# Retention heads in pairs: the turned results joined behind the next pair's steps, one inverse root for two heads

## The chip, the cores and the metric

The kernel runs on one core of one Trainium2 chip. The metric is the device time of one execution in microseconds (us). Before the change it is 2228.16 us, the median of three runs (2228.16, 2228.16 and 2229.72 us). About 0.2% of it, 4.5 us, is what a measurement of this kernel can tell from no change.

## The reference

One decoder layer over 256 tokens of width 2048: a half feed-forward, two token mixers side by side (retention and windowed attention), a second half feed-forward, and a gated embedding, each closed by a layer norm. The change lies in the retention mixer. What it computes:

```python
def reference(x, p, positions, ln_g, ...):
...
        rq = rotary(rq.reshape(B, S, RET_HEADS, RET_DK), positions, RET_DK, RET_THETA)
        rk = rotary(rk.reshape(B, S, RET_HEADS, RET_DK), positions, RET_DK, RET_THETA) * (RET_DK ** -0.5)
        rv = rv.reshape(B, S, RET_HEADS, RET_DV)
        ro = head_group_norm(retention_chunkwise(rq, rk, rv), ret_gn_g[i]).astype(h.dtype)
        ret_branch = (jax.nn.silu(rg) * ro) @ w_ret_out[i]
...
# retention_chunkwise: o_t = sum_{s<=t} gamma_h^(t-s) (q_t . k_s) v_s
...
def head_group_norm(o, g):
    B, S = o.shape[0], o.shape[1]
    mu = jnp.mean(o, axis=-1, keepdims=True)
    var = jnp.mean(jnp.square(o - mu), axis=-1, keepdims=True)
    y = (o - mu) * lax.rsqrt(var + GN_EPS)
    return y.reshape(B, S, -1) * g.astype(jnp.float32)
```

There are 8 retention heads; a head has 128 columns of query and key and 256 of value. Everything is float32.

## The kernel before, in words

Each matrix product is made exact by splitting: a weight chunk of 128 by 1024 numbers comes in by a DMA (`r...`, issued by SyncE), ScalarE rounds it to a high part (`h...`, L162), VectorE subtracts for the low part (`l...`, L164), and TensorE runs three matmuls for each product (L510 to L512): low times high, high times high, high times low. `fill` (L394) loads and splits chunks some way ahead of the chunk that TensorE is at; in the stage of this change the split is four chunks ahead.

Small work is laid between the chunks. `side` is a list of jobs, and `run_side` (L445) takes one job off it behind each chunk, after `fill` has issued the splits. The same call moves `lazy` on, which here prepares sums of later weights (`uf_gu`, `vf_gu`, L372 to L384), and `slow`, which makes a table of angles (`rota`, `triga`). Every engine runs its instructions in the order in which this code issues them, so a job's place in `side` is its place in each engine's queue.

The retention stage walks over four blocks of the gate (L1566, h = 0, 2, 4, 6). A block is one call of `paired_out` (L652): eight chunks of `w_in_f2`, summed into the two banks `rg`. Behind these 32 chunks the heads' jobs run. For a head h:

- `ret1` (L1475): TensorE multiplies queries and keys into the bank `rs`; VectorE multiplies by the decay into `rsc` (L1483, L1484).
- `ret1b` (L1488): ScalarE and VectorE split `rsc` into `rsp` (L113, L114).
- `ret2` (L1495): TensorE multiplies `rsp` by the values into the bank `ro`, nine matmuls (L1504); VectorE takes mean and variance into `gmv` (L1511, L1512).
- `ret2b` (L1516): `rsqrt` (L688), ten small instructions of VectorE, makes the inverse root; two more (L1525) write the normed head to `ron`.

For a pair c of heads:

- `ret2c`: VectorE multiplies `ron` by the gate (L1533).
- `ret3`: ScalarE copies the words of `ron` apart (`wro`, L227). `ret3a`: SyncE issues the DMA transpose `mro` (L231).
- `ret3b` (L1543): ScalarE joins what the transpose delivered into `ron0t`, `ron1t` and so on (L238) and scales it by the norm's weight (L1552); VectorE makes the low part (L1553). The results `rett` are first read at 1237.6 us of the span, by the output product of the retention branch, over 220 us after the last of them is written.

In `side` a pair of heads takes ten places: five for `ret1` to `ret2b`, and five for `ret2c`, `ret3`, `ret3a`, an empty one and `ret3b`, ahead of the next pair's five. A block takes off eight. So the list falls two further behind with every block: `ret1` of head 2 comes behind the sixth chunk of the second block, that of head 4 behind the last chunk of the third, and the jobs of the last pair run beside the value chunks `av` and the first attention features `aqk`.

PSUM has eight banks, taken in turn (L82); a block and its pair ask for six: two `rg`, two `rs`, two `ro`.

Of the kernel before, what the change touches and what calls it, by code (L numbers as in the profile page):

```python
# [8 lines left out]
F32 = mybir.dt.float32  # L9
# [4 lines left out]
ALU = mybir.AluOpType  # L14
PSUM = bass.MemoryType.PSUM

P = 128
# [3 lines left out]
HR, DK, DV = 8, 128, 256  # L21
# [4 lines left out]
GN_EPS = 1e-5  # L26
# [44 lines left out]
def layer(ctx: ExitStack, tc: tile.TileContext, io):  # L71
    nc = tc.nc
    sync, act, dve, pool, pe = nc.sync, nc.scalar, nc.vector, nc.gpsimd, nc.tensor
# [4 lines left out]
    small = ctx.enter_context(tc.tile_pool(name="small", bufs=3))  # L78
# [6 lines left out]
    def banks(name):  # L85
        return [bank(name + str(j)) for j in range(2)]

    def slot(shape, dt, name):
        return slots.tile(shape, dt, tag="slot", name=name)
# [351 lines left out]
    side = []  # L441
    lazy, slow = [], []
    idle = lambda: None
# [244 lines left out]
    def rsqrt(dst, var, n, eps):  # L688

        v = small.tile([P, 2, n], F32, tag=f"nv{n}", name="nv")
        dve.scalar_tensor_tensor(
            v, var[:, None, :].broadcast_to([P, 2, n]), eps, newton[:, :, None].broadcast_to([P, 2, n]),
            ALU.add, ALU.mult,
        )
        s = small.tile([P, n], I32, tag=f"ns{n}", name="ns", bufs=2)
        dve.tensor_scalar(s, v[:, 0].bitcast(I32), 1, None, ALU.logical_shift_right)
        y = small.tile([P, n], I32, tag=f"ny{n}", name="ny", bufs=2)
        dve.tensor_scalar(y, s, -1.0, float(0x5F3759DF - 2**31), ALU.mult, ALU.add)  # L700

        def square(cur, w, name):
            b = small.tile([P, n], F32, tag=f"nb{n}", name=name)
            if n == 1:
                dve.tensor_scalar(b, cur, cur, w, ALU.mult, ALU.mult)
            else:
                dve.tensor_tensor(b, cur, cur, ALU.mult)
                dve.tensor_tensor(b, b, w, ALU.mult)
# [634 lines left out]
    def mixers(ht, norm, residual, keepers, away):  # L1343
# [123 lines left out]
        for blk in range(2, 4):  # L1467
            ps = banks(f"rv{blk}")
# [4 lines left out]
        keep = {}  # L1473
# [21 lines left out]
        def ret2(h):  # L1495
            def f():
                s = keep.pop(("s", h))
                v = [x[:, :, h % 2 * DV : h % 2 * DV + DV] for x in rv[h // 2]]
                ps = bank(f"ro{h}").rearrange("p (a b) -> p a b", a=2)
                for t, blks in ((0, ((0, 0),)), (1, ((P, 0), (S, 1)))):  # L1500
                    for col, tk in blks:
                        at = slice(col, col + P)
                        for a, b in ((1, 0), (0, 0), (0, 1)):
                            pe.matmul(  # L1504
                                ps[:, t, :DV], s[:, a, at], v[b][:, tk],
                                start=(a, tk) == (1, 0) and col != S, stop=b == 1 and (t, col) in ((0, 0), (1, S)),
                            )
                st = small.tile([P, 2, 6], F32, tag="gst", name=f"gst{h}")
                mv = small.tile([P, 2, 2], F32, tag="gmv", name=f"gmv{h}")
                for t in range(2):  # L1510
                    dve.bn_stats(st[:, t], ps[:, t, :DV])  # L1511
                    dve.bn_aggr(mv[:, t], st[:, t])  # L1512
                keep["m", h] = ps, mv
            return f

        def ret2b(h):  # L1516
            def f():
                ps, mv = keep.pop(("m", h))
                rs = small.tile([P, 2], F32, tag="grs", name=f"grs{h}")
                rsqrt(rs, mv[:, :, 1], 2, GN_EPS)  # L1520
                if h % 2 == 0:
                    keep["o", h // 2] = slot([P, 2, 512], F32, f"ron{h}")
                o = keep["o", h // 2][:, :, h % 2 * DV : h % 2 * DV + DV]
                for t in range(2):
                    dve.tensor_scalar(  # L1525
                        o[:, t], ps[:, t, :DV], mv[:, t, 0:1], rs[:, t : t + 1], ALU.subtract, ALU.mult
                    )
            return f

        def ret2c(c):  # L1530
            def f():
                o = keep.pop(("o", c))
                dve.tensor_tensor(o, o, gate_v[c], ALU.mult)  # L1533
                keep["t", c] = Turn(o, f"ro{c}")
            return f

        def ret3(c):
            return lambda: keep["t", c].part()

        def ret3a(c):  # L1540
            return lambda: keep["t", c].move()

        def ret3b(c):  # L1543
            def f():
                raw = slot([P, 4, S], F32, f"ron{c}t")
                keep.pop(("t", c)).join(raw)
                for j in range(4):
                    if j % 2 == 0:
                        ret_t.append(slot([P, 2, 512], F32R, f"rett{len(ret_t)}"))
                    gk = gn[:, 4 * c + j : 4 * c + j + 1]  # L1550
                    hi, lo = ret_t[-1][:, j % 2, :S], ret_t[-1][:, j % 2, S:]
                    act.mul(hi, raw[:, j], gk)  # L1552
                    dve.scalar_tensor_tensor(lo, raw[:, j], gk, hi, ALU.mult, ALU.subtract)  # L1553
            return f

        both = lambda a, b: lambda: (a(), b())

        def two_heads(h):
            side.append(ret1(h))
            side.append(both(ret1b(h), ret1(h + 1)))  # L1560
            side.append(both(ret1b(h + 1), ret2(h)))
            side.append(both(ret2b(h), ret2(h + 1)))
            side.append(ret2b(h + 1))

        two_heads(0)
        for h in range(0, HR, 2):  # L1566
            ps = banks(f"rg{h}")
            paired_out(("w_in_f2", grp), KD, rhs, ps)
            grp += 2
            g = slot([P, 2, 512], F32, f"rgs{h}")  # L1570
            for t in range(2):
                act.activation(g[:, t], ps[t], AF.Silu)
            gate_v.append(g)
            c = h // 2
            side.extend((ret2c(c), ret3(c), ret3a(c), idle, ret3b(c)))
            if h + 2 < HR:
                two_heads(h + 2)
        aq = [slot([P, 4, S], F32, f"aq{j}") for j in range(2)]
        akv = slot([P, 4, S], F32, "akv")
        ps = banks("av")  # L1580
# [119 lines left out]
        for j in range(4):  # L1700
# [6 lines left out]
            ps = banks(f"gt{j}")  # L1707
# [26 lines left out]
        for j in range(4):  # L1734
            v = sig[4 + j]
# [8 lines left out]
        for b in range(2):  # L1744
# [3 lines left out]
            for n in range(2):  # L1748
                j = 2 * b + n
# [31 lines left out]
        ps = banks("mo2")  # L1781
# [4 lines left out]
        ps = banks("mo3")  # L1786
# [326 lines left out]
```

## Time and profile before

| What | Value |
|---|---|
| Median of three runs | 2228.16 us |
| The profiled execution's own time | 2227.58 us |
| Its span, from the first to the last instruction | 2225.5 us |
| TensorE (PE) busy | 2210.3 us, 99% of the span |
| VectorE (DVE) busy | 2027.8 us, 91% |
| ScalarE (ACT) busy | 1473.8 us, 66% |
| DMA, mean over the span | 259 GB/s |
| The retention stage (first `rg` to last `rg` matmul) | 865.8 to 970.0 us |

The profiled execution's time is 2.1 us over its span. With TensorE busy for 99% of the span, a change of the time is one of two things: TensorE waits less or more, or its clock is granted differently. Both are read by stage, since sums over the span hide them.

### The profile page before, as it was taken

To read this page: it belongs to the slowest core of one execution; us is meant where nothing else is said; L and a number is where in the kernel's file an instruction comes from. 1 tells how busy PE (TensorE), PEld (TensorE's weight loads), DVE (VectorE), ACT (ScalarE), POOL (GpSimd) and SP (SyncE) were. 2 spreads that over 40 slices of the span, in tenths; PEclk is the share of its full clock that TensorE was granted. 3 is DMA by queue.
4 is the path that set the end of the run, shared out by engine and by line. 5 is a ranking of instruction groups with operands and counts; after the bars stand their busy time and mean duration, and the time that the engine had idled before them with its cause. 6 is when DMAs were issued, how large, how long until landed. Compare 5 with 4: busy or idle time off the path is not lost.

```text
span 2225.5 us, 28896 instructions
## 1 busy us (share of the span) xinstructions
PE 2210.3 (99%) x9980; PEld 1826.6 (82%) x9980; DVE 2027.8 (91%) x2660; ACT 1473.8 (66%) x1706; POOL 48.3 (2%) x62
## 2 busy tenths in 40 slices
PE   9999999999999999999999999999999999999998
PEld 7888888888888888888788888888888878888887
DVE  6999999999988997999999888779999999999877
ACT  5877777777565555657866567466767678765553
POOL 0000000000000000000000000000000000000000
PEclk9999999999999999999999999999999999999999
DMA  9979889977686789876976578888899899767771
GB/s 315 275 224 267 248 245 262 251 234 245 217 304 234 254 272 317 260 279 227 295 235 221 183 210 327 311 302 261 292 311 309 293 261 274 216 238 240 282 289 71
DMA packets 315754, 576.00 MB, mean 259 GB/s; under 512 B 107084, under 2 KB 112076, under 8 KB 315608
## 3 DMA queue, kind: packets, MB, share of 16 engines
q1 hardware_dynamic: 305992, 543.79, 73.1%
q0 software_dynamic: 7632, 27.79, 6.7%
q10 hardware_dynamic: 1984, 2.58, 0.3%
q8 instruction: 78, 1.28, 0.2%
q14 instruction: 68, 0.56, 0.1%
HBM read 490.20 MB, written 33.55 MB: 235 GB/s over the span
## 4 chain that ended last, share of the span: by engine, by line
PE 87%; DVE 5%; DMA 4%; ACT 2%; issue 2%; SPq 0%; ACTq 0%; DVEq 0%; POOLq 0%
PE f2g L510 2%; PE f2g L511 2%; PE f2g L512 2%; PE f1g L512 2%; PE f1g L511 2%; PE f1g L510 2%; PE f1u L511 2%; PE f1u L512 2%; PE f1u L510 2%; PE f2u L512 2%; PE f2u L510 2%; PE f2u L511 2%; PE aqk L461 2%; PE f1d L511 1%; PE f1e L510 1%
## 5 line engine op out<-in xcount | busy, mean ns | idle before, releaser
L164 DVE TENSOR_TENSOR lf_gu<-rf_gu,hf_gu 128x1024 fp32r<-128x1024 f32 x123 | 145.2, 1218 | 18.9 <-ACT hf_gu L162 18.1
L164 DVE TENSOR_TENSOR lw_in_f<-rw_in_f,hw_in_f 128x1024 fp32r<-128x1024 f32 x124 | 148.6, 1218 | 10.3 <-ACT hw_in_f L162 9.5
L162 ACT CAST hf_gu<-rf_gu 128x1024 fp32r<-128x1024 f32 x123 | 123.6, 1049 | 26.5 <-DMA rf_gu<-in_f_gu 24.9
L164 DVE TENSOR_TENSOR lf_down<-rf_down,hf_down 128x1024 fp32r<-128x1024 f32 x96 | 115.8, 1219 | 24.5 <-ACT hf_down L162 19.1
L284 ACT CAST huf_gu<-uf_gu 128x1024 fp32r<-128x1024 f32 x83 | 87.3, 1052 | 76.4 <-DVE uf_gu L280 68.9
L293 ACT CAST hvf_gu<-vf_gu 128x1024 fp32r<-128x1024 f32 x83 | 87.5, 1054 | 76.1 <-DVE vf_gu L289 65.2
L162 ACT CAST hw_in_f<-rw_in_f 128x1024 fp32r<-128x1024 f32 x124 | 125.3, 1048 | 7.1 <-DMA rw_in_f<-in_w_in_f 3.3
L162 ACT CAST hf_down<-rf_down 128x1024 fp32r<-128x1024 f32 x96 | 98.5, 1050 | 30.4 <-DMA rf_down<-in_f_down 12.3
L298 DVE TENSOR_TENSOR lvf_gu<-vf_gu,hvf_gu 128x1024 fp32r<-128x1024 f32 x83 | 100.9, 1216 | 0.0
L296 DVE TENSOR_TENSOR luf_gu<-uf_gu,huf_gu 128x1024 fp32r<-128x1024 f32 x83 | 100.9, 1215 | 0.0
L287 DVE TENSOR_TENSOR lf_gu<-rf_gu,hf_gu 128x1024 fp32r<-128x1024 f32 x83 | 100.9, 1215 | 0.0
L277 ACT CAST hf_gu<-rf_gu 128x1024 fp32r<-128x1024 f32 x83 | 86.8, 1045 | 9.8 <-DMA rf_gu<-in_f_gu 6.7
L510 PE MATMUL f1g<-hf_gu,xt 128*128 128x512 f32 x223 | 87.0, 390 | 0.5 <-ACT hf_gu L113 0.5
L512 PE MATMUL f1g<-lf_gu,xt 128*128 128x512 f32 x223 | 87.1, 391 | 0.1
L511 PE MATMUL f1g<-hf_gu,xt 128*128 128x512 f32 x223 | 86.8, 389 | 0.0
L510 PE MATMUL f2g<-hf_gu,ht 128*128 128x512 f32 x196 | 76.4, 390 | 0.0
L512 PE MATMUL f2g<-lf_gu,ht 128*128 128x512 f32 x196 | 76.3, 389 | 0.0
L511 PE MATMUL f2g<-hf_gu,ht 128*128 128x512 f32 x196 | 76.3, 389 | 0.0
L510 PE MATMUL f1u<-hf_gu,xt 128*128 128x512 f32 x180 | 70.0, 389 | 0.0
L512 PE MATMUL f1u<-lf_gu,xt 128*128 128x512 f32 x180 | 70.0, 389 | 0.0
L511 PE MATMUL f1u<-hf_gu,xt 128*128 128x512 f32 x180 | 70.0, 389 | 0.0
L182 POOL DMA_DIRECT2D lf_gu<-rf_gu x37 | 32.1, 869 | 1637.2 <-DMA rf_gu<-in_f_gu 1049.0
(1640 smaller groups left out, 7318.5 us busy)
## 6 DMA issues: line engine op xcount, KB each, us to landing
rf_gu<-in_f_gu SPq DMA_DIRECT2D x362, 512.0 KB
rf_down<-in_f_down SPq DMA_DIRECT2D x176, 512.0 KB
rw_in_f<-in_w_in_f SPq DMA_DIRECT2D x148, 512.0 KB
lf_gu<-rf_gu POOLq DMA_DIRECT2D x37, 512.0 KB, 8.6
rw_rv<-in_w_rv SPq DMA_DIRECT2D x32, 512.0 KB
rw_ret<-in_w_ret SPq DMA_DIRECT2D x32, 512.0 KB
rw_mix<-in_w_mix SPq DMA_DIRECT2D x32, 512.0 KB
rw_pg<-in_w_pg SPq DMA_DIRECT2D x32, 512.0 KB
```

The lines of the kernel that those rows point to most:

```text
L162: act.copy(c.hi, c.raw)
L164: dve.tensor_tensor(c.lo, c.raw, c.hi, ALU.subtract)
L277: act.copy(a.hi, a.raw)
L284: act.copy(uh, u)
L287: dve.tensor_tensor(a.lo, a.raw, a.hi, ALU.subtract)
L293: act.copy(vh, v)
L296: dve.tensor_tensor(ul, u, uh, ALU.subtract)
L298: dve.tensor_tensor(vl, v, vh, ALU.subtract)
L461: pe.matmul(ps[f], hi[:, kk, f * P : (f + 1) * P], rhs(k), start=k == 0, stop=k == n_k - 1,)
L510: pe.matmul(o, al, bh, start=first, stop=False)
L511: pe.matmul(o, ah, bh, start=False, stop=False)
L512: pe.matmul(o, ah, bl, start=False, stop=self.left == 0)
```

## The change

`ret3b` of a pair no longer stands ahead of the next pair's steps. It goes into the last of the next pair's five places, together with the new `ret2b`. The empty place behind `ret3a` goes too, so that a pair takes eight places, as many as a block takes off. Only the last pair, which has no next one, keeps the empty place and `ret3b` behind it.

`ret2b` is called once for a pair: it waits until both heads' `ret2` are done, takes one inverse root of four columns where two of two columns were taken, and then norms both heads. The tile `gmv` holds both heads' means and variances.

```diff
                 st = small.tile([P, 2, 6], F32, tag="gst", name=f"gst{h}")
-                mv = small.tile([P, 2, 2], F32, tag="gmv", name=f"gmv{h}")
+                if h % 2 == 0:
+                    keep["v", h // 2] = small.tile([P, 4, 2], F32, tag="gmv", name=f"gmv{h}")
+                mv = keep["v", h // 2]
                 for t in range(2):
                     dve.bn_stats(st[:, t], ps[:, t, :DV])
-                    dve.bn_aggr(mv[:, t], st[:, t])
-                keep["m", h] = ps, mv
+                    dve.bn_aggr(mv[:, h % 2 * 2 + t], st[:, t])
+                keep["m", h] = ps
             return f
 
-        def ret2b(h):
+        def ret2b(c):
             def f():
-                ps, mv = keep.pop(("m", h))
-                rs = small.tile([P, 2], F32, tag="grs", name=f"grs{h}")
-                rsqrt(rs, mv[:, :, 1], 2, GN_EPS)
...
+                mv = keep.pop(("v", c))
+                rs = small.tile([P, 4], F32, tag="grs", name=f"grs{c}")
+                rsqrt(rs, mv[:, :, 1], 4, GN_EPS)
+                o = keep["o", c] = slot([P, 2, 512], F32, f"ron{c}")
+                for e in range(2):
+                    ps = keep.pop(("m", 2 * c + e))
+                    for t in range(2):
+                        j = 2 * e + t
+                        dve.tensor_scalar(
+                            o[:, t, e * DV : e * DV + DV], ps[:, t, :DV], mv[:, j, 0:1], rs[:, j : j + 1],
+                            ALU.subtract, ALU.mult,
+                        )
             return f
...
-        def two_heads(h):
+        def two_heads(h, last=idle):
             side.append(ret1(h))
             side.append(both(ret1b(h), ret1(h + 1)))
             side.append(both(ret1b(h + 1), ret2(h)))
-            side.append(both(ret2b(h), ret2(h + 1)))
-            side.append(ret2b(h + 1))
+            side.append(ret2(h + 1))
+            side.append(both(ret2b(h // 2), last))
...
-            side.extend((ret2c(c), ret3(c), ret3a(c), idle, ret3b(c)))
+            side.extend((ret2c(c), ret3(c), ret3a(c)))
             if h + 2 < HR:
-                two_heads(h + 2)
+                two_heads(h + 2, ret3b(c))
+            else:
+                side.extend((idle, ret3b(c)))
```

VectorE's queue around the first job of head 4 (`rsc4`), before. `lw_in_f2_12_7` is the low part of the third block's last chunk, `14_0` to `14_3` are chunks of the fourth block, `rett2` and `rett3` belong to `ret3b` of heads 2 and 3, `uf2_gu` and `vf2_gu` are the sums of later weights:

```order
L164 TENSOR_TENSOR lw_in_f2_12_7_8296<-rw_in_f2_12_7_8129,hw_in_f2_12_7_8295 128x1024
L164 TENSOR_TENSOR lw_in_f2_14_0_8317<-rw_in_f2_14_0_8172,hw_in_f2_14_0_8316 128x1024
L372 TENSOR_TENSOR uf2_gu_4_0_4_8326<-rf2_gu_4_0_4_8217,rf2_gu_4_1_4_8219 128x512
L373 TENSOR_TENSOR uf2_gu_4_0_4_8326<-rf2_gu_4_1_4_8219 128x512
L164 TENSOR_TENSOR lw_in_f2_14_1_8351<-rw_in_f2_14_1_8238,hw_in_f2_14_1_8350 128x1024
L164 TENSOR_TENSOR lw_in_f2_14_2_8369<-rw_in_f2_14_2_8277,hw_in_f2_14_2_8368 128x1024
L1553 SCALAR_TENSOR_TENSOR rett2_8377<-ron1t_8374,gn_79,rett2_8377 128x256 x2
L1553 SCALAR_TENSOR_TENSOR rett3_8382<-ron1t_8374,gn_79,rett3_8382 128x256 x2
L376 TENSOR_TENSOR vf2_gu_4_0_4_8327<-rf2_gu_4_0_4_8217,uf2_gu_4_0_4_8326 128x512
L377 TENSOR_TENSOR vf2_gu_4_0_4_8327<-vf2_gu_4_0_4_8327,rf2_gu_4_0_4_8217 128x512
L164 TENSOR_TENSOR lw_in_f2_14_3_8403<-rw_in_f2_14_3_8299,hw_in_f2_14_3_8402 128x1024
L1483 TENSOR_TENSOR rsc4_8411<-rs4_8408,dec2_7284 128x256
```

The same place of VectorE's queue after the change:

```order
L384 TENSOR_TENSOR lvf2_gu_3_0_5_8033<-vf2_gu_3_0_5_8029,hvf2_gu_3_0_5_8032 128x1024
L164 TENSOR_TENSOR lw_in_f2_12_7_8263<-rw_in_f2_12_7_8131,hw_in_f2_12_7_8262 128x1024
L1483 TENSOR_TENSOR rsc4_8271<-rs4_8268,dec2_7284 128x256
L1484 TENSOR_TENSOR rsc4_8271<-rs4_8268,dec2_7284 128x128
L164 TENSOR_TENSOR lw_in_f2_14_0_8287<-rw_in_f2_14_0_8191,hw_in_f2_14_0_8286 128x1024
L114 TENSOR_TENSOR rsp4_8292<-rsc4_8271,rsp4_8292 128x384
L1483 TENSOR_TENSOR rsc5_8298<-rs5_8295,dec2_7284 128x256
L1484 TENSOR_TENSOR rsc5_8298<-rs5_8295,dec2_7284 128x128
```

`rsc4` has moved up by four chunks, to right behind the split of `12_7`, and `rett2` and `rett3` no longer stand ahead of it.

ScalarE's queue at the same place, before (`ron1t` is the joining of heads 2 and 3, `rgs4` the gate of heads 4 and 5, `rsp4` the high part that head 4's second product needs):

```order
L162 CAST hw_in_f2_14_0_8316<-rw_in_f2_14_0_8172 128x1024
L162 CAST hw_in_f2_14_1_8350<-rw_in_f2_14_1_8238 128x1024
L162 CAST hw_in_f2_14_2_8368<-rw_in_f2_14_2_8277 128x1024
L238 COPY ron1t_8374<-mro1_8322 128x2x4x128 x2
L1552 ACTIVATE rett2_8377<-ron1t_8374,gn_79 128x256 x2
L1552 ACTIVATE rett3_8382<-ron1t_8374,gn_79 128x256 x2
L375 CAST huf2_gu_4_0_4_8328<-uf2_gu_4_0_4_8326 128x1024
L162 CAST hw_in_f2_14_3_8402<-rw_in_f2_14_3_8299 128x1024
L1572 ACTIVATE rgs4_8414<-rg40_8154 128x512
L1572 ACTIVATE rgs4_8414<-rg41_8155 128x512
L162 CAST hw_in_f2_14_4_8431<-rw_in_f2_14_4_8320 128x1024
L113 CAST rsp4_8437<-rsc4_8411 128x384
```

And after the change:

```order
L162 CAST hw_in_f2_14_0_8286<-rw_in_f2_14_0_8191 128x1024
L113 CAST rsp4_8292<-rsc4_8271 128x384
L162 CAST hw_in_f2_14_1_8327<-rw_in_f2_14_1_8221 128x1024
L113 CAST rsp5_8333<-rsc5_8298 128x384
L162 CAST hw_in_f2_14_2_8364<-rw_in_f2_14_2_8243 128x1024
L375 CAST huf2_gu_4_0_4_8305<-uf2_gu_4_0_4_8303 128x1024
L162 CAST hw_in_f2_14_3_8400<-rw_in_f2_14_3_8266 128x1024
L238 COPY ron1t_8429<-mro1_8245 128x2x4x128 x2
L1556 ACTIVATE rett2_8432<-ron1t_8429,gn_79 128x256 x2
L1556 ACTIVATE rett3_8437<-ron1t_8429,gn_79 128x256 x2
```

The joining of heads 2 and 3 now stands behind the splits of heads 4 and 5 instead of ahead of them.

More of the change, by code (lines that the diff above doesn't have):

```diff
@@ L1508, in f @@
                 st = small.tile([P, 2, 6], F32, tag="gst", name=f"gst{h}")
-                mv = small.tile([P, 2, 2], F32, tag="gmv", name=f"gmv{h}")
+                if h % 2 == 0:
+                    keep["v", h // 2] = small.tile([P, 4, 2], F32, tag="gmv", name=f"gmv{h}")
+                mv = keep["v", h // 2]
                 for t in range(2):
                     dve.bn_stats(st[:, t], ps[:, t, :DV])
-                    dve.bn_aggr(mv[:, t], st[:, t])
-                keep["m", h] = ps, mv
+                    dve.bn_aggr(mv[:, h % 2 * 2 + t], st[:, t])
+                keep["m", h] = ps
             return f
-        def ret2b(h):
+        def ret2b(c):
             def f():
-                ps, mv = keep.pop(("m", h))
-                rs = small.tile([P, 2], F32, tag="grs", name=f"grs{h}")
-                rsqrt(rs, mv[:, :, 1], 2, GN_EPS)
[L1521 to L1527, printed above, removed]
+                mv = keep.pop(("v", c))
[10 more added lines that the diff above has]
+                        )
             return f
```

## The prediction

> **What bounds the kernel now.** I read the page first, then who waited for whom on TensorE, then the timelines of TensorE, VectorE and ScalarE where the largest wait lies. The page says that TensorE is the bound:
>
> ```profile
> span 2225.5 us, 28896 instructions
> PE 2210.3 (99%) x9980; PEld 1826.6 (82%) x9980; DVE 2027.8 (91%) x2660; ACT 1473.8 (66%) x1706; POOL 48.3 (2%) x62
> ```
>
> So nothing that VectorE saves counts as such; it counts where TensorE waits. The waits of TensorE (total us, times, longest) hold one large entry, and it belongs to this stage: `ro` L1504 is `ret2`, `rsp` L114 is VectorE's half of `ret1b`.
>
> ```profile
> PE ro L1504 <- DVE rsp L114: 5.4, 2, 5.1
> PE f2u L512 <- DMA lf_gu<-rf_gu: 1.2, 1, 1.2
> ```
>
> TensorE's timeline shows what it cost (start, duration, instruction; in brackets the idle time before it). It is `ro` of head 4; 9 matmuls of 256 columns stand in a `ret2`.
>
> ```profile
> 944.87 0.39 PE L512 MATMUL rg<-lw_in_f,ht 128*128 128x512 f32 x1
> 950.35 0.80 PE L1504 MATMUL ro<-rvh,rsp 128*128 128x256 f32 x2 [5.09 <-DVE rsp L114]
> 953.27 0.40 PE L512 MATMUL rg<-lw_in_f,ht 128*128 128x512 f32 x1
> ...
> 955.33 0.39 PE L512 MATMUL rg<-lw_in_f,ht 128*128 128x512 f32 x1
> 956.63 0.40 PE L510 MATMUL rg<-hw_in_f,ht 128*128 128x512 f32 x1
> 957.10 0.39 PE L512 MATMUL rg<-lw_in_f,ht 128*128 128x512 f32 x1
> ```
>
> From the last matmul ahead of `ro` to the third behind it, 944.87 to 953.27, went 8.40 us. The same run of instructions for head 5, 955.33 to 957.10, took 1.77 us. So head 4's wait cost 8.40 - 1.77 = 6.63 us, more than the 5.09 us of idle time. The rest is the clock; the columns here are the stretch, busy time and count of PE, PEld, DVE, ACT, POOL, the granted clock, DMA share and GB/s:
>
> ```profile
> 945.30:949.80 4.50, 0.00 (x0) 0.00 (x0) 4.25 (x8) 4.50 (x7) 0.00 (x0) 1.00 1.00 365
> 949.90:953.20 3.30, 2.85 (x11) 2.75 (x12) 3.30 (x6) 3.27 (x5) 0.00 (x0) 0.50 1.05 403
> 953.30:970.30 17.00, 17.00 (x81) 14.23 (x80) 15.44 (x42) 5.01 (x7) 0.00 (x0) 1.00 0.73 276
> ```
>
> For some 3.3 us behind the wait the clock was halved: 11 matmuls took 953.27 - 950.35 = 2.92 us where head 5's took 1.53, so 1.4 us of the 6.63.
>
> Why `rsp` was late is read back along ScalarE, SyncE and VectorE:
>
> ```profile
> 933.09 2.00 ACT L227 COPY wro<-ron 128x1024 uint16<-128x1024 uint16 x2 [5.17 <-PE rg L512]
> 934.05 1.22 DVE L164 TENSOR_TENSOR lw_in_f<-rw_in_f,hw_in_f 128x1024 fp32r<-128x1024 f32 x1
> 935.11 3.20 SPq L231 DMA_TRANSPOSE mro<-wro  x1
> ...
> 940.48 2.56 ACT L238 COPY ron1t<-mro 128x1024 uint16<-128x1024 uint16 x2 [2.54 <-DMA mro<-wro]
> ...
> 943.07 1.71 ACT L1552 ACTIVATE rett<-ron1t,gn 128x256 fp32r<-128x256 f32 x4
> 943.62 1.69 DVE L1553 SCALAR_TENSOR_TENSOR rett<-ron1t,gn,rett 128x256 fp32r<-128x256 f32 x4 [2.85 <-ACT rett L1552]
> ...
> 947.84 0.42 DVE L1483 TENSOR_TENSOR rsc<-rs,dec 128x256 f32<-128x256 f32 x1
> ...
> 949.75 0.55 DVE L114 TENSOR_TENSOR rsp<-rsc,rsp 128x384 fp32r<-128x384 f32 x1
> ```
>
> The transpose of heads 2 and 3 is issued at 935.11 and joined from 940.48. `ret3b` stands two steps behind it, so ScalarE waited 2.54 us for the transfer, then worked 4.3 us on the joining (940.48 to 944.78), VectorE waited 2.85 us for ScalarE, and `rsc` of head 4, next in its queue, ran at 947.84 although TensorE had `rs` ready here:
>
> ```profile
> 919.24 0.40 PE L510 MATMUL rg<-hw_in_f,ht 128*128 128x512 f32 x1
> ...
> 938.30 0.59 PE L1479 MATMUL rs<-rq1t,rk1t 128*128 128x256 f32 x2
> 941.70 0.59 PE L1479 MATMUL rs<-rq1t,rk1t 128*128 128x256 f32 x2
> ```
>
> **The change part by part.** *`ret3b` moved behind the next pair's steps.* It takes ScalarE's 2.54 us wait and 4.3 us of work, and VectorE's 2.85 us wait and 1.69 us of work, out of the way of `rsc` and `rsp` of head 4: the 6.63 us go. `ret3b` then stands five steps behind its transpose. TensorE's rows give a step's length: 919.24 to 938.30 are seven chunks, 2.72 us each, and 938.30 to 941.70 is a chunk with `ret1`, 3.40 us. Five steps are over 14 us, against the 5.4 us from 935.11 to 940.48, so ScalarE no longer waits there. Its 4.3 us of work are hidden: chunks are split four ahead, 10.9 us, and the three steps that follow (`ret2c`, `ret3`, `ret3a`) feed nothing to TensorE. Without this cover it would cost up to 4.3 us a pair. No DMA is issued later: `ret3a`, which issues the transpose, comes behind the third chunk of every block, where the first pair's stands now and the later ones stand two steps or more behind.
>
> *One inverse root for two heads.* The ten instructions run from the first of these rows to the second, and 921.94 - 919.98 = 1.96 us with the pauses between them; the third row has four columns instead of two and takes as long.
>
> ```profile
> 919.98 0.15 DVE L693 SCALAR_TENSOR_TENSOR nv<-gmv,cst 128x4 f32<-128x4 f32 x1
> 921.94 1.00 DVE L1525 TENSOR_SCALAR ron<-ro,gmv,grs 128x256 f32<-128x256 f32 x2
> 1091.96 0.17 DVE L1616 TENSOR_TENSOR amx<-amx,sink 128x4 f32<-128x4 f32 x1
> ```
>
> Forty instructions go, 1.96 us of VectorE a pair. On TensorE's path this is worth nothing by itself; it counts in the next sum. `ro` of the first head of a pair stays in its bank until the joint `ret2b`; with six requests a pair out of eight banks, that bank comes round only eight requests later, over a block on: nothing, or, were it needed at once, a step, 2.7 us.
>
> *Eight steps a pair instead of ten.* This is the part that can give something back. `rsc` of head 4 now stands right behind the split of `12_7`, which is the row at 934.05 above; the next instruction could start at 935.2. What VectorE does ahead of that place is the same as before, less two inverse roots, 3.9 us. TensorE comes there sooner: with 919.24 plus three chunks it gives `rs` at 927.4, and wants `rsp` two steps of 3.40 later, at 934.2. From `rsc` to `ro` went 950.35 - 947.84 = 2.5 us. So `ro` can start between 935.2 - 3.9 + 2.5 = 933.8, no wait, and 935.2 + 2.5 = 937.7, a wait of 3.5 us: VectorE has next to no idle time in which to catch up, as the first row shows (55.99 of 58.20 us busy, the rest are short pauses). The next two rows are ScalarE's timeline, and the last is the split as the chain that ended last lists it.
>
> ```profile
> 877.00:935.20 58.20, 58.20 (x272) 48.57 (x272) 55.99 (x125) 29.39 (x37) 0.00 (x0) 1.00 0.84 280
> ...
> 891.58 0.58 ACT L1572 ACTIVATE rgs<-rg 128x512 f32<-128x512 f32 x1
> 892.06 1.05 ACT L162 CAST hw_in_f<-rw_in_f 128x1024 fp32r<-128x1024 f32 x1
> ...
> 893.81 1.22 DVE lw_in_f L164
> ```
>
> How much of the 3.9 us arrives? The gate's activation at 891.58 follows the block's last matmul, and the cast at 892.06 behind it ends at 893.11; the split at 893.81 needs that cast. VectorE can come there 0.7 us sooner, not 1.96: the first root loses 1.3 us to this wait. For the second I know no such row; I take half there too, so 2.0 of 3.9 us arrive and `ro` of head 4 waits 937.7 - 2.0 - 934.2 = 1.5 us. I choose the middle because one root has a row that halves it.
>
> A short wait keeps the clock, by the one other wait behind the start that passes a microsecond:
>
> ```profile
> 1831.60 0.50 PE L512 MATMUL f2u<-lf_gu,ht 128*128 128x512 f32 x1 [1.17 <-DMA lf_gu<-rf_gu]
> 1831.00:1833.00 2.00, 1.41 (x6) 1.19 (x7) 2.00 (x4) 1.00 (x2) 0.00 (x0) 1.00 0.75 196
> ```
>
> After 1.17 us idle the granted clock stayed 1.00; after 5.09 us it fell to 0.50. I price 1.5 us as idle time alone, and 3.5 us as idle time with or without the 1.4 us of halved clock. The Trainium skill, TensorE: Matmul & The Clock Gate, Part 1, says that the clock halves after at least one idle window of about 3.4 us, and that the window runs freely; by that rule 1.5 us costs no clock and 3.5 us may. Both waits above agree with it.
>
> *The other pairs.* The same sum for heads 2 and 3 starts at the first block's first matmul and at the split of the second block's last chunk:
>
> ```profile
> 865.76 0.39 PE L510 MATMUL rg<-hw_in_f,ht 128*128 128x512 f32 x1
> 903.85 1.22 DVE L164 TENSOR_TENSOR lw_in_f<-rw_in_f,hw_in_f 128x1024 fp32r<-128x1024 f32 x1
> ```
>
> A block is 25.3 us of TensorE: eight chunks, two `ret1` of 3.40 - 2.72 = 0.68, two `ret2` of 1.08 (1.77 less three matmuls of 0.23). With four chunks more `rs` of head 2 is out at 902.0, and `ro` is wanted at 908.8. VectorE is at that place at 905.0, or 1.96 sooner, and with 2.5 us of chain and two angle instructions between (0.8) `ro` can start at 906.3 to 908.3: no wait. Heads 6 and 7: the angle table is done by then, so VectorE has less to do in a block; 0, and at most the 0.32 us that this row shows for the last pair now.
>
> ```profile
> 983.54 0.51 PE L1504 MATMUL ro<-rvh,rsp 128*128 128x256 f32 x2 [0.32 <-DVE rsp L114]
> ```
>
> **The sum.** -6.63 + 1.5 = -5.1 us. The profiled execution took 2227.58 us, so 2222.5 us; it lies 0.6 us under the median of the three runs, and on the median the forecast is 2228.16 - 5.13 = 2223.0 us. The 5 us stay gained to the end if no weights are late afterwards, and TensorE's only wait for a transfer there is the 1.2 us of `f2u`.
>
> **The rivals.**
>
> *A longer wait at head 4.* VectorE keeps none of the saving: 3.5 us, 2228.16 - 6.63 + 3.5 = 2225.0, and with the halved clock 2226.4 us. For it: VectorE is full in this stretch. Against: the rows allow 0.7 us of the first root for sure. By the clock gate rule of the Trainium skill cited above, 3.5 us is just the length from which the clock may fall.
>
> *The time is lost again to transfers.* The wait let DMA run ahead (365 and 403 GB/s in the rows around it, 276 behind); without it a later chunk may be late by as much: 2228.2 us. Against: TensorE waits for no transfer in the retention and attention stages.
>
> *Slower: the denser steps put VectorE behind in every pair.* In the stretch up to 935.2 VectorE has 2.2 us of slack, and each pair's statistics, root and norm now fall into eight steps. If the deficit comes back at each of the three later pairs, each `ro` waits 3.5 us and the clock halves each time: 3 x (3.5 + 1.4) - 6.63 = +8.1, 2236.2 us. It decides from 2.2 us a pair (three times that is 6.63). For it: 91% of VectorE's time is taken. Against: the root saves 1.96 us a pair, and heads 2 and 3 have room.
>
> **How the numbers follow.** The forecast with its wait of 0 to 2.1 us: 0.70. The longer wait: 0.16. Lost to transfers: 0.08. Slower: 0.06. About 0.2%, 4.5 us, is what a measurement of this kernel can tell from no change, so faster means under 2223.7 us: the forecast is faster (0.70), the longer wait and the lost gain are within (0.24), the last is slower (0.06). The range goes from no wait at all, with the 0.32 us gone too and the 0.6 us between the runs (2228.16 - 6.95 - 0.6 = 2220.6), to the longer wait with halved clock, 2226.4 us.
>
> **What would show it.** Right: TensorE's wait list has lost the 5.1 us entry; ScalarE waits for no `mro` at L238 but for the last pair; `ro` of head 4 waits 0 to 2.1 us at a clock of 1.00; eighty small instructions of the root have become forty. Wrong: a wait of over 2.2 us at any `ro`, a halved clock between 865 and 990 us, or a new wait for a transfer or a split behind 990 us.

## The result and the profile after

The changed kernel takes 2222.43 us (median of nine runs, 2220.73 to 2223.73) where the kernel before takes 2228.40 us on the same chip (nine runs). The ratio is 0.9972, with a 95% interval of 0.9962 to 0.9982: between 4 and 8.5 us gained. The forecast was 2223.0 us.

The profiled execution took 2221.96 us. The page of the changed kernel:

```profile
span 2220.0 us, 28845 instructions
PE 2209.2 (100%) x9980; PEld 1825.5 (82%) x9980; DVE 2021.5 (91%) x2620; ACT 1475.5 (66%) x1706; POOL 48.4 (2%) x62
```

VectorE runs 2620 instructions instead of 2660, the forty of the root. Its busy time fell by 6.3 us, but TensorE's share of its span rose: the gain lies in what TensorE no longer waits for. TensorE's waits (total, times, longest):

```profile
PE f1g L510 <- ACT hf_gu L113: 1.4, 1, 1.4
PE f2u L512 <- DMA lf_gu<-rf_gu: 0.9, 2, 0.5
PE ro L1504 <- DVE rsp L114: 0.5, 1, 0.5
```

The entry of 5.1 us is gone, and 0.5 us is left of it. No transfer has taken its place: `f2u` waited 1.2 us before and 0.9 us now. The 1.4 us at `f1g` lie at the start of the kernel, far ahead of the change; the list of before has 0.5 us there.

Where the time came from is best read between two marks of TensorE's timeline: the first `rg` matmul and the first `ga0a` matmul, the first of the gate behind the attention steps. The first mark of before stands at 865.76, as shown above; its second:

```profile
1144.17 0.50 PE L510 MATMUL ga0a<-hw_in_f,ht 128*128 128x512 f32 x1
```

The changed kernel's marks, with the two rows between which head 4's wait lies:

```profile
866.14 0.39 PE L510 MATMUL rg<-hw_in_f,ht 128*128 128x512 f32 x1
...
934.23 0.39 PE L512 MATMUL rg<-lw_in_f,ht 128*128 128x512 f32 x1
935.15 0.51 PE L1504 MATMUL ro<-rvh,rsp 128*128 128x256 f32 x2 [0.53 <-DVE rsp L114]
...
1138.17 0.50 PE L510 MATMUL ga0a<-hw_in_f,ht 128*128 128x512 f32 x1
```

From mark to mark it was 1144.17 - 865.76 = 278.41 us, and it is 1138.17 - 866.14 = 272.03 us: 6.38 us gained between them. Ahead of the marks the profiled run lost 866.14 - 865.76 = 0.38 us, and behind them (2220.0 - 1138.17) - (2225.5 - 1144.17) = 0.50 us. So the spans differ by 6.38 - 0.38 - 0.50 = 5.50 us. The 6.38 us are 6.63 for head 4's old wait, less 0.53 for the new one, and 0.32 for the last pair's, which is gone: 6.42.

The clock was granted in full throughout the stage. These are the two windows around head 4; the stretches ahead of them from 865 us and behind them to 1138 us read 1.00 as well. The columns are again stretch, busy time and count of PE, PEld, DVE, ACT, POOL, granted clock, DMA share and GB/s:

```profile
917.70:944.00 26.30, 25.77 (x124) 21.48 (x123) 25.68 (x53) 16.67 (x21) 0.00 (x0) 1.00 0.75 243
944.00:970.40 26.40, 26.40 (x136) 22.47 (x135) 25.00 (x53) 19.33 (x26) 0.00 (x0) 1.00 0.92 315
```

VectorE's timeline around the place that the prediction was about:

```profile
931.75 1.22 DVE L164 TENSOR_TENSOR lw_in_f<-rw_in_f,hw_in_f 128x1024 fp32r<-128x1024 f32 x1
932.88 0.42 DVE L1483 TENSOR_TENSOR rsc<-rs,dec 128x256 f32<-128x256 f32 x1
933.22 0.28 DVE L1484 TENSOR_TENSOR rsc<-rs,dec 128x128 f32<-128x128 f32 x1
...
934.55 0.55 DVE L114 TENSOR_TENSOR rsp<-rsc,rsp 128x384 fp32r<-128x384 f32 x1
```

`rsc` of head 4 stands behind the split of `12_7` with no pause between, VectorE's half of `rsp` follows the next split, whose row stands between these and is not shown, and is done at 935.10, and `ro` starts at 935.15. ScalarE's half was done at 933.58 + 0.51 = 934.09. So what is left of the wait is VectorE's queue, and neither ScalarE nor a transfer. ScalarE's timeline shows the joining where it stands now, with no wait for `mro`:

```profile
933.58 0.51 ACT L113 CAST rsp<-rsc 128x384 fp32r<-128x384 f32 x1 [2.69 <-DVE rsc L1484]
...
939.99 2.57 ACT L238 COPY ron1t<-mro 128x1024 uint16<-128x1024 uint16 x2
```

### The profile page after: what moved, and what is told of

Same layout as the page of the kernel before. It is cut to its first block, busy times and chain, and to the rows that moved or that the text cites. A ratio compares the mean times of both kernels' runs of the same rounds, so it can differ in the third digit from the quotient of the medians.

```text
span 2220.0 us, 28845 instructions
## 1 busy us (share of the span) xinstructions
PE 2209.2 (100%) x9980; PEld 1825.5 (82%) x9980; DVE 2021.5 (91%) x2620; ACT 1475.5 (66%) x1706; POOL 48.4 (2%) x62
## 4 chain that ended last, share of the span: by engine, by line
PE 94%; DMA 3%; DVE 2%; ACT 1%; issue 1%; SPq 0%; ACTq 0%; DVEq 0%
PE f1g L510 3%; PE f1g L512 3%; PE f1g L511 3%; PE f2g L510 2%; PE f1u L511 2%; PE f1u L510 2%; PE f1u L512 2%; PE f2g L511 2%; PE f2g L512 2%; PE f2u L512 2%; PE f2u L510 2%; PE f2u L511 2%; PE aqk L461 2%; PE f1e L512 1%; PE f2d L510 1%; PE f1d L512 1%
```

## The experiments

Two things were changed at once, and with them the number of places. The theory: `ret3b` ahead of the next pair held up ScalarE and VectorE, and through them head 4; the move takes that away, but with eight places a pair TensorE comes sooner than VectorE, and the joint root gives VectorE back most of that. The rivals: one of the two parts does it alone; or the denser steps are the gain; or they are a loss. The edits are shown against the changed kernel, and of each the lines that matter.

**The move without the joint root.** The root, norm and tile `gmv` as before the change, the order as after it (the lines of `two_heads`; the rest is the old `ret2` and `ret2b`):

```diff
-            side.append(ret2(h + 1))
-            side.append(both(ret2b(h // 2), last))
+            side.append(both(ret2b(h), ret2(h + 1)))
+            side.append(both(ret2b(h + 1), last))
```

> The move alone: the joining stands behind the next pair's steps, eight places a pair, but each head takes its own inverse root as before. My theory (the move takes away the wait of 5.1 us and its halved clock, the joint root pays for the denser steps): VectorE keeps nothing of the 3.9 us, so the first job of head 4 stands at 935.2 us of the span of before; with the 2.3 us that the changed kernel's trace shows from there to ro, ro starts at 937.5 where TensorE wants it at 934.2: a wait of 3.3 us at head 4, perhaps one of up to 2 us at head 6. Time 2228.4 - 6.9 + 3.3 = 2224.8 us, up to 2226.8 with the second wait, and 1.4 more if a wait of this length halves the clock. Rival 'the order alone does it': no wait over 0.6 us, 2222.4 us as the whole change. Rival 'the root alone does it': 2228.4 us, as before.

Measured: 2226.49 us (11 runs, 2224.42 to 2228.11; the kernel before, on the same chip as this and the next three, 2228.65 us, 29 runs), ratio 0.999, interval 0.9982 to 0.9999. Its wait list and the window behind the wait:

```profile
PE ro L1504 <- DVE rsp L114: 3.1, 2, 3.0
```

```profile
937.47:940.88 3.41, 1.33 (x10) 1.33 (x11) 3.41 (x8) 2.28 (x4) 0.00 (x0) 1.00 0.74 190
940.88:944.30 3.42, 3.42 (x10) 2.64 (x9) 3.35 (x8) 2.60 (x4) 0.00 (x0) 0.50 1.01 350
```

The move alone leaves 3.0 us at the same `ro`, and the clock was halved behind it. The profiled run, 2228.11 us, is the slowest of the eleven: its retention stage began at 867.87 us, some 2 us later than in the kernel before (865.76), so these 2 us were lost ahead of everything that the move touches. In the timelines of this run the place of `rsc` can be set against the stage's start:

```profile
867.87 0.39 PE L510 MATMUL rg<-hw_in_f,ht 128*128 128x512 f32 x1
```

```profile
937.28 0.42 DVE L1483 TENSOR_TENSOR rsc<-rs,dec 128x256 f32<-128x256 f32 x1
```

That is 937.28 - 867.87 = 69.41 us behind the start; in the changed kernel it is 932.88 - 866.14 = 66.74. The joint root is worth 2.67 us to VectorE there.

**The joint root without the move.** `ret3b` and the empty place ahead of the next pair, ten places, as before:

```diff
...
-            side.extend((ret2c(c), ret3(c), ret3a(c)))
+            side.extend((ret2c(c), ret3(c), ret3a(c), idle, ret3b(c)))
             if h + 2 < HR:
-                two_heads(h + 2, ret3b(c))
-            else:
-                side.extend((idle, ret3b(c)))
+                two_heads(h + 2)
```

> The joint root alone: ten places a pair and the joining ahead of the next pair's steps, as before. My theory: VectorE reaches the norm of heads 2 and 3 sooner by the 2.7 us that arrived in the changed kernel; the turned copy, the transpose and the joining start sooner by as much, so head 4's wait shrinks from 5.1 to about 2.4 us, and being short it leaves the clock at 1.00: 2228.4 - 2.7 - 1.4 = 2224.3 us (2223 to 2226). ScalarE still waits about 2.5 us for the transpose at the joining. Rival 'the order alone does it': 2228.4 us, the wait of 5.1 us unchanged, since the transfer and not VectorE sets it. Rival 'the root alone does it': 2222.4 us.

Measured: 2224.3 us (11 runs, 2222.86 to 2227.31), ratio 0.9981, interval 0.9972 to 0.999. Its largest wait and the windows:

```profile
PE ro L1504 <- DVE rsp L114: 2.6, 1, 2.6
```

```profile
944.78:948.19 3.41, 0.83 (x6) 0.67 (x6) 3.26 (x8) 3.41 (x6) 0.00 (x0) 1.00 1.04 402
948.19:951.60 3.41, 3.41 (x12) 2.86 (x11) 3.38 (x6) 3.41 (x5) 0.00 (x0) 0.50 1.03 410
```

The wait is 2.6 us instead of 5.1: so again 2.5 us of VectorE's saving arrive. That a wait of this length leaves the clock alone was wrong for the profiled run. The runs differ: in three of the eleven the mean granted clock was 1.000 (median span 2221.8 us), in five 0.998 (2223.3 us). One halved stretch of 3.41 us lowers the mean over 2223 us by 0.0008, so the three had none of that length, and the five had one or more: 0.998, being rounded, takes at least 6.7 us at half clock (2 x 0.0015 x 2223), and the halved stretch at the end of the program holds 1.2 to 4.1 us of the span in the profiles. Where in the span the five had it is not known, and two of them (2221.9 and 2222.1 us) were no longer than the three.

**The move with ten places.** The move and the old root, and two empty places put back (shown against the run with the move alone):

```diff
             if h + 2 < HR:
+                side.extend((idle, idle))
                 two_heads(h + 2, ret3b(c))
```

> The move without the denser steps: the joining behind the next pair's steps, two empty places put back so that a pair takes ten, separate roots. My theory: TensorE asks for head 4's product no sooner than before, and nothing waits for the transpose ahead of it, so the wait at head 4 is gone though VectorE is not relieved: 2228.4 - 6.9 = 2221.5 us (2220.5 to 2223). Rival 'the denser steps bring the gain' (the last pair no longer runs beside the value chunks and attention): 2228 us. Rival 'VectorE's load decides': a wait of over 2 us at head 4, 2224 us or more.

Measured: 2222.3 us (7 runs, 2221.62 to 2223.88), ratio 0.9972, interval 0.9961 to 0.9983. Two rows of its wait list:

```profile
PE as L1608 <- DVE aq L1297: 1.0, 1, 1.0
...
PE ro L1504 <- DVE rsp L114: 0.2, 1, 0.2
```

With ten places the move needs no joint root at head 4. By the medians it gains as much as the whole change. What is new is the wait of 1.0 us at `as`, the attention's first product, for VectorE. The kernel before has ten places too and no such wait, and the run with both parts and ten places (below) has none either; what made VectorE late there was not tested.

**Eight places without the move.** The joint root, with `ret3b` in one step with the next pair's `ret1`, one step behind its transpose:

```diff
-            side.append(ret1(h))
+            side.append(both(last, ret1(h)))
...
-            side.append(both(ret2b(h // 2), last))
+            side.append(ret2b(h // 2))
```

> Eight places a pair and the joint root, but the joining is not moved behind: it stands in one step with the next pair's first job, one step behind its transpose. My theory: ScalarE waits for the transpose in every pair and VectorE behind it. In the changed kernel's trace the turned copy ends at 927.7; 5.4 us of transpose and 4.3 us of joining later VectorE makes its low part and only then the first job, about 938.1; ro follows 2.3 us later, 940.4, where 934.2 is wanted: a wait of some 6 us with a halved clock at head 4, and waits of some 3 to 7 us at heads 2 and 6. Time between 2222.4 + 10 and 2222.4 + 21: 2232 to 2243 us, slower than before. Rival 'the denser steps or the root bring the gain': 2222.4 us, since both are kept.

Measured: 2232.47 us (11 runs, 2231.18 to 2234.25), ratio 1.0018, interval 1.001 to 1.0027, so slower than before. Its wait list, ScalarE's and VectorE's timelines:

```profile
PE ro L1504 <- DVE rsp L114: 8.0, 3, 4.2
```

```profile
932.60 2.56 ACT L238 COPY ron1t<-mro 128x1024 uint16<-128x1024 uint16 x2 [2.34 <-DMA mro<-wro]
```

```profile
935.73 1.68 DVE L1557 SCALAR_TENSOR_TENSOR rett<-ron1t,gn,rett 128x256 fp32r<-128x256 f32 x4 [2.51 <-ACT rett L1556]
937.33 0.42 DVE L1483 TENSOR_TENSOR rsc<-rs,dec 128x256 f32<-128x256 f32 x1
```

It is the chain of the kernel before, only denser: ScalarE waits for the transfer, VectorE for ScalarE, `rsc` stands behind both. Now heads 2, 4 and 6 wait 0.7, 4.2 and 3.0 us, where before head 4 waited 5.1 us and the last pair 0.3. Eight places are no gain in themselves.

**Both parts with ten places.** The changed kernel with the same two empty places put back.

> The change whole (joint root, scaling behind the next pair's steps), but with two idle places put back, so that a pair has ten places again. Theory (the first step of the next pair must not come before VectorE is through with the last pair; the move gives that in ten steps, the root's saving gives it nearly in eight): the 0.53 us wait of the changed kernel at head 4's ro is gone and no other wait takes its place, no halved clock: 2221.9 us (2220.8 to 2223), that is 0 to 1 us under the changed kernel's 2222.43 and within 1 us of the move with ten steps, 2222.3. Rival (the ten places push the last pair's retention work into the attention steps, as in the move with ten steps, where as waited 1.0 us): 2223 us, with a wait of about 1 us at as L1608. If the joint root still earned something by itself there, it would be under 2221.

Measured: 2221.39 us (7 runs, 2220.49 to 2222.8), ratio 0.9969, interval 0.9958 to 0.9981. The head of its wait list, in which neither `ro` nor `as` appears:

```profile
PE warm L1998 <- POOL ident masks.py:199: 1.4, 1, 1.4
PE f2u L512 <- DMA lf_gu<-rf_gu: 1.3, 2, 1.0
PE f1g L512 <- DVE lf_gu L164: 0.4, 1, 0.4
```

To compare it with the changed kernel on one chip, both ran once more:

> The changed kernel as it is, beside the next run on the same chip: 2222.4 us (2221.5 to 2223.3), with the wait of about 0.5 us at ro of head 4 and no halved clock.

> The change with ten places a pair once more, beside the changed kernel on the same chip. Theory: 0.5 to 1 us less than the changed kernel (its wait of 0.53 us, and what the pauses around it cost), 2221.4 to 2221.9. Rival: the same time within 0.3 us, since the wait only moves.

The changed kernel took 2221.9 us (6 runs, 2220.84 to 2223.45; ratio to before 0.9972, interval 0.996 to 0.9983), the one with ten places 2220.95 us (5 runs, 2220.07 to 2221.78; 0.9964, 0.9951 to 0.9978). It was lower by 1.0 us both times, but the runs overlap and the intervals too. The wait is shown to be gone; by the medians a gain of about a microsecond is likely and not proven. The marks in the timelines, in the table below, show it for the stage.

**More work for VectorE at head 4.** The changed kernel with `rsc` of head 4 written five times:

```diff
-                dve.tensor_tensor(s[:, :S], ps[:, 0, :S], d[:, :S], ALU.mult)
+                for _ in range(5 if h == 4 else 1):
+                    dve.tensor_tensor(s[:, :S], ps[:, 0, :S], d[:, :S], ALU.mult)
```

> The changed kernel with rsc of head 4 written five times instead of once, that is four more VectorE instructions of 128x256 at the place in VectorE's queue on which the residual wait hangs, 4 x 0.33 = 1.3 us by the pitch of L1483. Theory (VectorE's place at rsc of head 4 sets when ro can start; what VectorE is given there comes out as a wait of the same size): ro of head 4 waits 0.5 + 1.3 = 1.8 us. That is under the 2.1 us of idle time in one window from which a halved clock was seen, so the clock stays at 1.00, and the kernel takes 1.3 us more than the changed one, about 2223.7 us. Rival (another engine or a transfer sets the residual wait, and VectorE has room): the wait stays within 0.3 us of 0.53. If a later pair's ro takes a wait as well, VectorE has no room to catch up within a pair.

Measured: 2222.67 us (one run). TensorE's timeline, VectorE's, and the windows:

```profile
936.28 0.50 PE L1505 MATMUL ro<-rvh,rsp 128*128 128x256 f32 x2 [2.35 <-DVE rsp L114]
```

```profile
932.18 2.25 DVE L1484 TENSOR_TENSOR rsc<-rs,dec 128x256 f32<-128x256 f32 x5
934.35 0.28 DVE L1485 TENSOR_TENSOR rsc<-rs,dec 128x128 f32<-128x128 f32 x1
```

```profile
931.70:935.11 3.41, 2.23 (x10) 1.50 (x8) 3.27 (x8) 0.39 (x1) 0.00 (x0) 1.00 0.81 246
935.11:938.52 3.41, 2.24 (x14) 2.07 (x15) 3.41 (x7) 2.79 (x5) 0.00 (x0) 1.00 0.98 271
```

From the first `rsc` to the half behind it went 934.35 - 932.18 = 2.17 us, where the changed kernel took 933.22 - 932.88 = 0.34: 1.83 us more, not the 1.3 expected (0.46 us for each where I had 0.33; the reason is open). The wait grew by 2.35 - 0.53 = 1.82 us, the same amount. So VectorE's place at `rsc` sets the wait of head 4, as the theory has it. No later pair waited, and the clock stayed at 1.00. The one run lies 0.8 us over the changed kernel's median on the same chip (2221.9 us), not 1.8; single runs of one kernel differ by up to 3 us here, so its whole time neither supports nor contradicts that. The stage itself does. These are the first `rg` and the first `ga0a` matmul in the timeline of each profiled run:

| Kernel | First `rg` | First `ga0a` | Between, us |
|---|---|---|---|
| Before | 865.76 | 1144.17 | 278.41 |
| Changed | 866.14 | 1138.17 | 272.03 |
| Changed, once more | 865.72 | 1137.71 | 271.99 |
| Move alone, eight places | 867.87 | 1144.50 | 276.63 |
| Joint root alone, ten places | 865.58 | 1141.03 | 275.45 |
| Move alone, ten places | 865.95 | 1138.62 | 272.67 |
| Eight places, joint root, not moved | 865.69 | 1148.99 | 283.30 |
| Both parts, ten places | 865.45 | 1136.51 | 271.06 |
| Both parts, ten places, once more | 865.83 | 1136.89 | 271.06 |
| Changed, `rsc` of head 4 five times | 865.45 | 1139.27 | 273.82 |

The two clock probes of the next part, which are the changed kernel up to the second mark, have 272.02 and 272.01. So one kernel repeats within 0.04 us here, and much smaller differences can be read than from whole runs. The four extra instructions cost 273.82 - 272.03 = 1.79 us of TensorE's time, as much as the wait grew. Both parts with ten places take 0.9 to 1.0 us less than the changed kernel, and TensorE is busy for all of the 271.06 us both times: for this stage the gain is shown. Against the kernel before, the whole change gains 6.38 us between the marks, the move with ten places 5.74, the joint root alone 2.96, and the move alone with eight places 1.78, the last two with a halved clock each.

**From what wait on the clock is halved.** Two kernels answer this, the changed one with eight stalls of graded length each, put between the chunks of `ma` through `side`:

```diff
+            pause, spare = slot([P, 1024], F32, f"pause{j}"), bank(f"pz{j}")
+            pool.memset(pause, 0.0)
+
+            def stall(n, pause=pause, spare=spare):
+                pe.transpose(spare[:, :P], pause[:, :P], ident)
+                for w in [512] * (n // 2) + [256] * (n % 2):
+                    pool.memset(pause[:, :w], 0.0)
+                pe.transpose(spare[:, P : 2 * P], pause[:, :P], ident)
+
+            for n in STALLS[2 * j : 2 * j + 2]:
+                side.extend((idle, lambda n=n, f=stall: f(n)))
             pa = banks(f"ma{j}")
```

`STALLS` is (5, 8, 6, 9, 7, 10, 8, 6) in the first and (8, 5, 10, 7, 6, 9, 7, 4) in the second.

> The changed kernel with eight stalls of TensorE of graded length put in the stage of ma, where TensorE otherwise waits for nothing: a transpose reads a tile of zeros, GpSimd sets the tile to zero anew 2.5 to 5 times (512 columns each), a second transpose waits for that. The stalls are some 1.6, 2.4, 1.85, 2.7, 2.15, 2.9, 2.4 and 1.85 us, 5.4 us of matmuls or more apart. Theory A (the clock halves only when a window of 3.4 us is idle as a whole): no halved clock at any of them, and the kernel is longer by the idle time alone, about 18 us. Theory B (a share of a window near two thirds is enough): all stalls of up to 1.9 us keep a clock of 1.00, those of 2.1 to 2.9 us are followed by a halved clock in some cases, always for 3.41 us, each of which costs 1.7 us more. Theory C (any stall over 1.5 us halves the clock): eight halvings.

> The same with the stalls in another order, some 2.4, 1.6, 2.9, 2.15, 1.85, 2.7, 2.15 and 1.3 us. Theory A: no halved clock. Theory B: none up to 1.9 us, some from 2.1 us on, and where the same length halves the clock in one probe and not in the other, the place of the stall in the window decides. Theory C: seven halvings.

Measured: 2250.37 and 2253.95 us (one run each). The clock was halved four times in the first and five times in the second. In the first, the halved stretches began at 1235.00, 1262.31, 1272.55 and 1282.79 us: 8, 3 and 3 times 3.413 us apart, each 3.41 us long; the one at the end of the program began at 2245.34 us, 282 times 3.413 us behind the last of these. So in these runs the clock changes on a fixed grid of 3.413 us. That idle time is counted by window of that grid is what the probes test. The windows view of the first probe, cut along it:

```profile
1231.59:1235.00 3.41, 1.26 (x7) 0.74 (x5) 2.87 (x5) 0.00 (x0) 1.85 (x4) 1.00 0.66 210
1235.00:1238.42 3.42, 3.12 (x8) 2.54 (x9) 2.20 (x5) 2.05 (x3) 1.14 (x2) 0.50 0.59 162
1241.83:1245.24 3.41, 1.60 (x9) 1.08 (x8) 2.16 (x2) 0.35 (x1) 1.58 (x3) 1.00 0.34 128
1245.24:1248.65 3.41, 3.41 (x16) 2.81 (x16) 0.00 (x0) 0.00 (x0) 0.00 (x0) 1.00 0.14 19
1248.65:1252.07 3.42, 1.71 (x9) 1.11 (x7) 2.47 (x4) 0.00 (x0) 1.48 (x3) 1.00 0.78 292
1252.07:1255.48 3.41, 2.31 (x11) 1.92 (x12) 2.16 (x6) 1.63 (x2) 1.83 (x4) 1.00 0.00 1
1255.48:1258.89 3.41, 3.41 (x17) 2.72 (x15) 2.74 (x3) 3.41 (x5) 0.00 (x0) 1.00 0.40 145
```

A window idle for 3.41 - 1.26 = 2.15 us was followed by a halved one; windows idle for 1.81, 1.71 and 1.10 us were not. The last two of these belong to one stall of 2.82 us that a window's edge divided. In the second probe a stall of the same length fell into one window but for 0.25 us. The two rows of TensorE's timelines, first probe and second:

```profile
1253.17 0.33 PE L1751 MATMUL pz<-ident,pause 128*128 128x128 f32 x1 [2.82 <-POOL pause L1750]
```

```profile
1275.77 0.47 PE L1751 MATMUL pz<-ident,pause 128*128 128x128 f32 x1 [2.82 <-POOL pause L1750]
```

and the second probe's windows there:

```profile
1272.10:1275.51 3.41, 0.85 (x5) 0.41 (x3) 3.32 (x6) 0.65 (x1) 2.21 (x5) 1.00 0.00 0
1275.51:1278.92 3.41, 3.15 (x8) 2.57 (x9) 3.41 (x5) 1.45 (x2) 1.11 (x2) 0.50 0.00 0
```

The same stall of 2.82 us halved the clock here, with 2.56 us idle in one window, and not there. So the length of the stall alone does not decide. Theories A and C fall, B holds. Over all profiles, among the windows that were not followed by a halved clock the longest idle times were 1.76 and 1.81 us; among those that were, the shortest were 2.08 (the move alone, above), 2.11 and 2.15 us. The limit lies between 53% and 61% of a window. The last 10 us of the program are left out of this: there the clock also fell behind windows with 1.5 to 1.7 us of idle time, which hold a few matmuls of other shapes whose ends the profile models. Why is open.

## Why the prediction was right, and where it was off

*What bounds the kernel, and the 6.63 us.* Right. The wait is gone when `ret3b` is out of the way and VectorE is in time (the move with ten places), it shrinks by VectorE's saving when `ret3b` stays (the root alone), and waits come in three pairs when `ret3b` stays and the steps are denser. TensorE's side came out exactly: `ro` of head 4 was wanted at 934.2, and in the changed kernel the matmul ahead of it ended at 934.23 + 0.39 = 934.62, with the stage begun 0.38 us later.

*The residual wait at head 4, +1.5 us.* The mechanism was right (the dose of VectorE work came out one for one), its size was too large: 0.53 us measured. Two numbers of the sum were off. I took 2.0 of the root's 3.9 us to arrive; 2.67 did, so 3.92 - 2.67 = 1.25 us were lost. The 2.0 did not follow from my own rows either: 0.7 for the first root, which is a third of 1.96 and not half, and half for the second, 0.98, make 1.7, and with that the sum would have had a wait of 1.8 us. Part of what was lost is a cause that I had left out. In the changed kernel VectorE waits in three places where the run with the move alone, which has the old root, has no wait: for TensorE's `ro` ahead of the statistics of heads 1 and 3, and for the cast that I had named:

```profile
880.75 0.43 DVE L1513 BATCH_NORM_STATS2 gst<-ro 128x6 f32<-128x256 f32 x1 [0.39 <-PE ro L1504]
...
893.23 1.23 DVE L164 TENSOR_TENSOR lw_in_f<-rw_in_f,hw_in_f 128x1024 fp32r<-128x1024 f32 x1 [0.44 <-ACT hw_in_f L162]
...
914.23 0.43 DVE L1513 BATCH_NORM_STATS2 gst<-ro 128x6 f32<-128x256 f32 x1 [0.21 <-PE ro L1504]
```

That is 0.39 + 0.44 = 0.83 us in the first pair, where I had 1.3 for the cast alone, and 0.21 us in the second, where I had half of the root without a row: 1.04 of the 1.25 us; the remaining 0.2 us is not accounted for. The choice of the middle of the range was a guess that lay near. And from `rsc` to `ro` went 935.15 - 932.88 = 2.27 us, not 2.5. With both, 1.5 - 0.67 - 0.23 = 0.6 us. My end of the range without any saving was right: I had VectorE's place at 935.2 - 865.76 = 69.44 us behind the stage's start, and the move without the joint root had it at 69.41. That eight places are the part that gives something back was right too: with ten places the stage is 0.9 to 1.0 us shorter.

*The other terms.* ScalarE waits no longer for `mro` ahead of the next pair; heads 2, 3, 6 and 7 wait for nothing; the 0.32 us of the last pair went. Four columns of the inverse root take as long as two, as I had assumed: the joint root's rows run from 882.97 to 884.95 us, 1.98 us, against 1.96 for one head's root before.

```profile
882.97 0.16 DVE L693 SCALAR_TENSOR_TENSOR nv<-gmv,cst 128x8 f32<-128x8 f32 x1
...
884.95 1.90 DVE L1528 TENSOR_SCALAR ron<-ro,gmv,grs 128x256 f32<-128x256 f32 x4
```

So the stage gained 6.4 us where 5.1 were forecast, and 0.9 us of that were lost at other places of the profiled runs, at the start and behind 1138 us. That the forecast for the whole kernel, 0.6 us from the median, came closer than its parts is luck: the wait was sized 1.0 us too long and the last pair's 0.3 us was not counted as gained, and the 0.9 us lost elsewhere, which were not in the sum, made up for most of it.

*The price of a short wait.* Half right. No wait of the changed kernel was long enough to matter. But I read from one wait of 1.17 us and one of 5.09 us that the clock falls somewhere near 3.5 us. By the probes it can fall from 2.1 us on, if the wait lies within one window, and it did fall behind 2.6 and 3.0 us in the runs of the two parts alone. The Trainium skill, TensorE: Matmul & The Clock Gate, Part 1, has the window right (3413 ns, running freely) and puts the fall behind an idle window; the traces differ from it there, since a window idle for 2.08 of its 3.41 us was enough. My rival of a longer wait, 2225.0 without and 2226.4 us with the halved clock, met its counterpart in the move alone: 3.0 us with a halved clock, and 278.41 - 276.63 = 1.78 us gained between the marks, where the rival had 2228.16 - 2226.4 = 1.76.

*The rivals.* The time was not lost again to transfers: `f2u` waits 0.9 us. The slower outcome was real, but not for this change: it needs `ret3b` to stay in front, as the kernel with eight places and no move shows, +3.8 us by the medians (+4.9 between the marks) where I had priced 8.1. Two of its later pairs waited 4.2 and 3.0 us with a halved clock behind each, and head 2 only 0.7.

## What to carry to other kernels

Work that waits for a transfer belongs behind the work that another engine is waiting for, and its place in each in-order queue counts for more than its length: 4.3 us on ScalarE and 1.7 us on VectorE cost TensorE nothing once they stood behind the next pair's splits and the pair had ten places. When steps are packed closer, set the time at which each engine comes to its place against the time at which it is wanted; a saving on an engine that is nearly full counts in just that difference, and here two thirds of it arrived. By these traces a wait of more than 2 us on TensorE should be priced with up to 1.7 us of halved clock besides (half of 3.41), which comes or not by where the wait lies. And a small gain is better read between two marks of the timeline, where this stage repeated within 0.04 us, than from whole runs, which differ by up to 3 us.

## What was not expected of the hardware

- The granted clock is decided on a grid of 3.413 us. It was halved for the next window when a window held 2.08 us of idle time or more, and not at 1.81 us or less, the last 10 us of the program left out; a stall of 2.35 us that a window's edge cut in halves (1.18 and 1.17 us) left it at 1.00.
- The same kernel is granted a different mean clock from run to run: the joint root alone had 1.000 in three runs of eleven and 0.998 in five, and their median spans differ by 1.5 us, though the groups overlap. That the grid lies differently to the same wait in each run would explain it; this was not shown run by run.
